# A two-layer decoder trunk on one core: first loads in another order and partly held back, last product in three parts, one selector matmul per forgetting head

## The chip, the cores and the metric

One core of one Trainium2 chip. The metric is the device time in microseconds (us) of one execution, the median of the runs shown. One execution was also taken by the hardware profiler; all views below come from it. Engines are named as in the profile: PE (TensorE matmul) and PEld (its weight load), DVE (VectorE), ACT (ScalarE), POOL (GpSimd), SP (SyncE, which issues DMAs).

## The reference, cut to what matters

Inputs are float32; 256 tokens (`SEQ`), width 2048 (`D_MODEL`), two layers. Each layer adds a mixer and an MLP to the residual `x`.

```python
def reference(x, ...):
    for i in range(2):
        h = rms_norm(x, mix_norm_g[i])
        # layer 0: forgetting attention, 16 heads of 128; layer 1: dilated attention, 8 heads x 3 groups
        mix = fox_attention(h, ...) if i == 0 else dilated_attention(h, ...)
        x = x + mix
        h = rms_norm(x, mlp_norm_g[i])
        x = x + sq_relu_mlp(h, mlp_w_up[i], mlp_w_down[i])      # (relu(h @ up) ** 2) @ down, d_ff 8192

def fox_attention(h, w_in, b_f, q_gain, k_gain, w_out):
    q, k, v, f = jnp.split(h @ w_in, [2048, 4096, 6144], axis=-1)    # f: one column per head
    q, k = rms_norm(q, q_gain), rms_norm(k, k_gain)                  # per head
    c = jnp.cumsum(jax.nn.log_sigmoid(f + b_f), axis=1)
    s = q @ k.T * 128 ** -0.5 + c[query] - c[key]                    # per head, causal
    return (softmax(s) @ v) @ w_out
```

## The kernel before, in words

**Products.** Every matrix product has float32 accuracy by parts: a weight tile is cast to a rounded part `wh` (ACT, line 279) and a remainder `wl` (DVE, line 280), the activations `hT` likewise (lines 370, 371), and `product` (lines 297 to 315) issues three matmuls for each of 16 `k` (128 rows of the contraction) and each of two blocks of 128 tokens: high by high, high by low, low by high (lines 308, 309, 310), each 128x128 by 128x512. One product is 96 matmuls over 512 output columns. `product_transposed` does the MLP's up half with swapped operands.

**Weights.** `plan` lists all weight tiles in order of use, 256 rows by 512 columns (512 KB, two `k`). `load` issues one DMA for each on SP's queue into one of five `raw` buffers, `split` casts it into one of five `wh`/`wl` pairs. After every second `k`, `product` calls `split` for a tile five ahead, so the streams run ahead of PE by a fixed depth.

**Order.** `Jobs` runs generators at ticks (one tick per `k`). A generator issues a step, yields a number of ticks or a key, and so is woven between matmuls. `behind(...)` holds instructions back in a scheduler's order until others are issued. The scheduler of the framework then fixes one instruction order per engine; each engine works strictly in that order.

**Start.** `load_x` brings `x` in four chunks of 512 columns (`xt[0..3]`), the first in two halves by columns. `gain_rows` and `gain_columns` bring the norm's gains and turn them to columns with one PE transpose. `norm_chain` for tag `n0`, for each chunk: four transposes for each half chunk (line 365, tile `ptx_n`), then ACT and DVE make the two parts of `hT` from PSUM with the gains (two PSUM buffers `ps_tp`, so the third group waits for the first to be read), and later ACT squares `x` for the row sums (line 381) that give `rstd`. The row scale is put on behind the product. `wake` issues idle transposes on PE. `more_constants` brings the forget-gate columns `wf` (128x16 rows of 64 bytes, line 160), the bias and the other gains. `rest` fills the weight pipeline. The first product is q of heads 0 to 3; then `gate` (line 522, tile `pf`), then k, then v. `gate_chain` turns the gate's sums into `c_q` and `negc`, the negated cumulative sums by head, as two parts on partitions 0 to 15 and 32 to 47.

**Forgetting heads.** `fox_head` builds a head's scores in one PSUM bank: columns 0 to 127 for the first token block (queries 0 to 127, 128 keys), columns 128 to 383 for the second (256 keys). Each block is its score matmuls (`scores`, lines 504 and 507) plus one matmul of a selector `sel` by `negc` (line 596), which adds the head's -c to all rows.

**End.** The last product (`out_proj` of the last MLP block, n = 3) runs both token blocks side by side through all 16 `k`; then `add_chain` adds each block to `x` (line 694) and `store` writes 256 KB for each block on SP's queue (line 708).

Of the kernel before, what the change touches and what calls it, by code (L numbers as in the profile page):

```python
# [17 lines left out]
P = 128  # L18
# [69 lines left out]
def trunk(ctx: ExitStack, tc, x, fox_w_in, fox_b_f, fox_q_gain, fox_k_gain, fox_w_out, dil_w_in,  # L88
# [34 lines left out]

    def gain_rows(name, sources):
        rows = work.tile([2 * KC, P], F32, tag="s", name=name, bufs=4)
        at = 0
        for src in sources:
            nc.sync.dma_start(rows[at:at + src.shape[0], :], src)
            at += src.shape[0]
        return rows[0:at, :]  # L130
# [6 lines left out]

    per_chunk = "l (c p) -> (l c) p"
    mix_rows = gain_rows("g_mix", [mix_norm_g.rearrange(per_chunk, p=P)])


# [15 lines left out]
    def more_constants():  # L157
        yield 6
        wf = work.tile([P, KC, FH], F32, tag="t2", name="wf")
        nc.sync.dma_start(wf, fox_w_in[0][:, 3 * D:3 * D + FH].rearrange("(c p) n -> p c n", p=P))  # L160
        nc.sync.dma_start(bf, fox_b_f.to_broadcast([P, FH]))
        qk_rows = gain_rows("g_qk", [fox_q_gain, fox_k_gain, dil_q_gain[0], dil_k_gain[0]])
        mlp_rows = gain_rows("g_mlp", [mlp_norm_g.rearrange(per_chunk, p=P)])
# [79 lines left out]
    def behind(*instructions):  # L243
# [3 lines left out]
        return stack  # L247

    state = {"raw": 0, "split": 0}
    raws, splits = [], []  # L250

    def load():
        i = state["raw"]
        if i >= len(plan):
            return
        w, r, cols = plan[i]
        t = wpool.tile([P, RAW_SUB, NC], F32, tag="raw", name=f"raw{i}", bufs=RAW_BUFS)
        at = 0
        for c, width in cols:
            nc.sync.dma_start(  # L260
                t[:, :, at:at + width],
                w[r:r + RAW_SUB * P, c:c + width].rearrange("(c p) n -> p c n", p=P),
            )
            at += width
        raws.append(t)
        state["raw"] += 1

    def split():
        i = state["split"]
        per = RAW_SUB // W_SUB  # L270
        if i >= len(plan) * per:
            return
        if i % per == 0:
# [4 lines left out]
        with behind(*(issued.get("n0", []) if i < 2 * W_BUFS else [])):  # L278
            nc.scalar.copy(hi, raw)  # L279
            nc.vector.tensor_sub(lo, raw, hi.bitcast(F32))  # L280
        splits.append((hi, lo))
# [4 lines left out]
    def in_turn(w, apart=NC // 2):  # L286
        return w.rearrange("p (b h n) -> p b n h", n=apart, h=2)
# [9 lines left out]
    def product(keys, lhs, post):  # L297

        acc = [ps_acc.tile([P, NC], F32, tag="acc", name=f"acc{used[0]}_{t}") for t in range(NT)]
        for k in range(KC):  # L300
# [13 lines left out]
            jobs.tick()  # L314
        jobs.spawn(post(acc))

    def product_transposed(keys, both, banks, post):
# [38 lines left out]
    def norm_chain(tag, col, n, ssp, wait, later):  # L356
        yield wait
        for half in range(2):
            pr = n * 2 + half
            pt = ps_tp.tile([P, 2, S], F32, tag="tp", name=f"ptx_{tag}_{pr}")  # L360
            with behind(*([issued["product"]] if wait else [])):
                for i in range(2):
# [12 lines left out]
            jobs.done.add((tag, pr))  # L375
            yield min(wait, 1)
        yield later
        with behind(issued[tag, n * 2 + 1][0]):
            for t in range(NT):
# [120 lines left out]

    def scores(ps, t, q, k, i, stop):
        (q_whole, q_hi, q_lo), (k_whole, k_hi, k_lo) = q, k
        if t == 0:
            nc.tensor.matmul(ps[:, 0:P], q_whole[:, i, :], k_whole[:, i, :], start=True, stop=stop)
            return
        for x, (a, b) in enumerate(((q_hi, k_hi), (q_hi, k_lo), (q_lo, k_hi))):
            nc.tensor.matmul(ps[:, P:3 * P], a[:, i, :], in_turn(b[:, i, :], P // 2), start=x == 0, stop=stop and x == 2)

# [6 lines left out]
    c_q = const.tile([P, NT, FH], F32, name="c_q")  # L515
    negc = const.tile([P, S], F32R, name="negc")

# [7 lines left out]
    def gate_chain(tag, pf):  # L525
# [50 lines left out]
        nc.vector.tensor_scalar(ct, pct, -1.0, None, ALU.mult)  # L576
        zero = work.tile([P, S], F32, tag="s", name="g_zero", bufs=4)
        nc.vector.memset(zero, 0.0)
        nc.vector.tensor_copy(negc, zero)
        nc.vector.tensor_copy(negc[0:FH, :], ct)  # L580
        nc.vector.tensor_sub(negc[32:32 + FH, :], ct, negc[0:FH, :].bitcast(F32))
        jobs.done.add("gate")

    def fox_head(j, hh, qT, kT, vt, sel):
# [5 lines left out]
        yield 2 * hh + 2  # L590
        ps = ps_sc.tile([P, 512], F32, tag="sc", name=f"sc_f{h}")
        for t in range(NT):
            at = ps[:, t * P:t * P + (t + 1) * P]
            n = (t + 1) * P
            scores(ps, t, qT[hh // 2], kT[hh // 2], hh % 2, False)
            nc.tensor.matmul(at, sel[:, hh, :], negc[:, 0:n], start=False, stop=True)
        s = work.tile([P, 3 * P], F32, tag="s", name=f"s_f{h}", bufs=4)
# [38 lines left out]
    def dil_head(q4, i, qTs, kTs, vt):  # L636
# [5 lines left out]
        for g in range(3):  # L642
            yield ("table", g)
            ps = ps_sc.tile([P, 512], F32, tag="sc", name=f"sc_d{h}_{g}")
            for t in range(NT):
                scores(ps, t, qTs[g], kTs[g], i, True)
            slope = 2.0 ** (-8.0 * (g * DH + h + 1) / N_SLOPES)
# [41 lines left out]
    def add_chain(acc, n, then, ready, scale):  # L689
# [11 lines left out]
        yield 0  # L701

    def out_proj(keys, lhs, then=None, ready=None, scale=None):
        for n in range(NX):
            product(keys, lhs, lambda acc, n=n: add_chain(acc, n, then, ready, scale))

# [48 lines left out]

    first = normed("n0", 0, lambda n: (0, 1, 4, 8)[n], lambda n: 11 - 3 * n)

    def load_x(n):
        step = NC if n else NC // 2
        for c in range(0, NC, step):  # L760
            nc.sync.dma_start(xt[n][:, :, c:c + step], xv[:, :, n * NC + c:n * NC + c + step])

    def rest():
        load_x(2)
        yield 2
        split()
        load_x(3)
        while state["split"] - used[0] < W_BUFS:
            split()
            yield 1  # L770

    load_x(0)
    gain_columns("g_mix", mix_rows, 0)
    jobs.spawn(first(0))
    with behind(issued["transposed"]):
        wake(12)
    for i in range(4):
        split()
        if i == 1:
            load_x(1)  # L780
    for n in range(1, NX):
# [64 lines left out]
```

## Time and profile before

| | |
|---|---|
| time, median of 3 runs | 2191.28 us (2191.07 to 2192.96) |
| the profiled execution | 2193.09 us, of which the span is 2191.4 us |
| mean granted PE clock | 0.998 |
| PE busy | 2179.7 us, 99% of the span |
| DVE busy | 1373.8 us, 63% |
| ACT busy | 1100.3 us, 50% |
| DMA | 425.76 MB, mean 194 GB/s |
| matmul 128x128 by 128x512, record / distance of starts | 0.38 us / 0.216 us |
| cast of one weight tile, ACT line 279 / DVE line 280 | 1.05 us / 1.23 us |

How to read it: a PE record overlaps the next one, so the work of PE is counted by the distance of starts. A timeline row gives start, duration, engine, line, operation, tiles, shape and count; at its end in brackets the idle time before it and who ended it. PEclk is the clock granted to PE as a share of full speed.

### The profile page before, as it was taken

The page shows a single profiled execution, that of the slowest core. Times are in us where ns is not written, and L with a number is a line of the kernel's source. Part 1 is how long each engine was busy: PE and PEld are TensorE (multiplying, and loading weights), DVE is VectorE, ACT ScalarE, POOL GpSimd, SP SyncE. Part 2 cuts the span into 40 slices and gives each one's busy share as a digit, 9 for nine tenths or more (in the row PEclk, how much of TensorE's full clock was granted, in tenths as well). Part 3 has the DMA queues.
Part 4 walks back from the last instruction along what each step waited for, and adds up shares of the span by engine and source line. Part 5 has one row for each costly group of instructions (what it writes and reads, how often), then busy time and mean ns, then how long its engine had stood idle before and what let it go on. Part 6 is the DMA issues. An engine that isn't in the chain of part 4 may idle for free.

```text
span 2191.4 us, 29887 instructions
## 1 busy us (share of the span) xinstructions
PE 2179.7 (99%) x11441; PEld 1939.3 (88%) x11441; DVE 1373.8 (63%) x1799; ACT 1100.3 (50%) x1516; POOL 48.2 (2%) x51
## 2 busy tenths in 40 slices
PE   8999999999999999999999999999999999999999
PEld 7888888998998998998888888888988988988988
DVE  6776686665565565565666767665655655665564
ACT  5655555554454454455555555555544544544442
POOL 1011000000000000000000000000000000000000
PEclk9999999999999999999999999999999999999999
DMA  7565556666766766765665565656666766666664
GB/s 228 170 192 173 182 167 200 197 202 203 202 203 203 201 203 203 201 202 194 192 200 174 178 189 172 199 175 189 206 203 201 202 202 202 201 203 203 201 212 144
DMA packets 248687, 425.76 MB, mean 194 GB/s; under 512 B 16792, under 2 KB 66528, under 8 KB 248544
## 3 DMA queue, kind: packets, MB, share of 16 engines
q1 hardware_dynamic: 248544, 423.86, 62.7%
q8 instruction: 89, 1.46, 0.3%
q14 instruction: 54, 0.44, 0.1%
HBM read 421.70 MB, written 2.10 MB: 193 GB/s over the span
## 4 chain that ended last, share of the span: by engine, by line
PE 98%; DVE 1%; DMA 0%; issue 0%; ACT 0%; SPq 0%; DVEq 0%; ACTq 0%
PE acc L308 21%; PE acc L309 21%; PE acc L310 21%; PE up_n1a_acc L329 5%; PE up_n3a_acc L329 5%; PE up_n1a_sc L329 3%; PE up_n1a_tp L329 3%; PE up_n3a_sc L329 3%; PE up_n3a_tp L329 3%; PE up_n3a_acc L333 3%; PE up_n1a_acc L333 3%; PE up_n3a_sc L333 1%; PE up_n3a_tp L333 1%; PE up_n1a_tp L333 1%; PE up_n1a_sc L333 1%; PE ptx_n L365 1%
## 5 line engine op out<-in xcount | busy, mean ns | idle before, releaser
L280 DVE TENSOR_TENSOR wl<-raw,wh 128x1024 fp32r<-128x1024 f32 x800 | 979.4, 1225 | 713.4 <-ACT wh L279 706.5
L279 ACT CAST wh<-raw 128x1024 fp32r<-128x1024 f32 x800 | 839.5, 1049 | 889.0 <-PE acc L310 528.5
L308 PE MATMUL acc<-wh,hT_n 128*128 128x512 f32 x896 | 347.1, 388 | 2.1 <-ACT wh L279 2.1
L309 PE MATMUL acc<-wl,hT_n 128*128 128x512 f32 x896 | 340.8, 380 | 0.1
L310 PE MATMUL acc<-wh,hT_n 128*128 128x512 f32 x896 | 340.7, 380 | 0.0
L308 PE MATMUL acc<-wh,aTh_n1a 128*128 128x512 f32 x512 | 194.5, 380 | 0.0
L309 PE MATMUL acc<-wl,aTh_n1a 128*128 128x512 f32 x512 | 194.0, 379 | 0.0
L310 PE MATMUL acc<-wh,aTl_n1a 128*128 128x512 f32 x512 | 194.0, 379 | 0.0
L308 PE MATMUL acc<-wh,aTh_n3a 128*128 128x512 f32 x512 | 194.0, 379 | 0.0
L309 PE MATMUL acc<-wl,aTh_n3a 128*128 128x512 f32 x512 | 194.0, 379 | 0.0
L310 PE MATMUL acc<-wh,aTl_n3a 128*128 128x512 f32 x512 | 194.0, 379 | 0.0
L310 PEld LDWEIGHTS acc<-wh,hT_n 128*128 128x128 f32 x896 | 169.9, 190 | 24.0
L308 PEld LDWEIGHTS acc<-wh,hT_n 128*128 128x128 f32 x896 | 169.9, 190 | 23.3 <-ACT wh L279 2.3
L309 PEld LDWEIGHTS acc<-wl,hT_n 128*128 128x128 f32 x896 | 170.2, 190 | 21.7 <-DVE wl L280 0.8
L329 PE MATMUL up_n3a_acc<-hT_n,wh 128*128 128x512 f32 x512 | 181.6, 382 | 0.0
L329 PE MATMUL up_n1a_acc<-hT_n,wh 128*128 128x512 f32 x512 | 181.6, 382 | 0.0
L333 PE MATMUL up_n1a_acc<-hT_n,wl 128*128 128x256 f32 x512 | 139.6, 273 | 0.0
L333 PE MATMUL up_n3a_acc<-hT_n,wl 128*128 128x256 f32 x512 | 139.6, 273 | 0.0
L310 PEld LDWEIGHTS acc<-wh,aTl_n1a 128*128 128x128 f32 x512 | 96.8, 189 | 13.7
L310 PEld LDWEIGHTS acc<-wh,aTl_n3a 128*128 128x128 f32 x512 | 96.8, 189 | 13.7
L309 PEld LDWEIGHTS acc<-wl,aTh_n3a 128*128 128x128 f32 x512 | 96.8, 189 | 13.7
L308 PEld LDWEIGHTS acc<-wh,aTh_n3a 128*128 128x128 f32 x512 | 96.8, 189 | 13.7
(721 smaller groups left out, 3161.4 us busy)
## 6 DMA issues: line engine op xcount, KB each, us to landing
raw<-in_mlp_w_up_dram SPq DMA_DIRECT2D x256, 512.0 KB, 4.4
raw<-in_mlp_w_down_dram SPq DMA_DIRECT2D x256, 512.0 KB, 4.1
raw<-in_fox_w_in_dram SPq DMA_DIRECT2D x96, 512.0 KB, 3.8
raw<-in_dil_w_in_dram SPq DMA_DIRECT2D x192, 256.0 KB, 3.1
raw<-in_fox_w_out_dram SPq DMA_DIRECT2D x32, 512.0 KB, 3.8
raw<-in_dil_w_in_dram SPq DMA_DIRECT2D x32, 512.0 KB, 3.8
raw<-in_dil_w_out_dram SPq DMA_DIRECT2D x32, 512.0 KB, 3.6
out_dram<-x SPq DMA_DIRECT2D x8, 256.0 KB, 5.6
```

Of the source, the lines that this page charges most:

```text
L279: nc.scalar.copy(hi, raw)
L280: nc.vector.tensor_sub(lo, raw, hi.bitcast(F32))
L308: nc.tensor.matmul(acc[t], ah[:, tok], hi, start=first, stop=False)
L309: nc.tensor.matmul(acc[t], ah[:, tok], lo, start=False, stop=False)
L310: issued["product"] = nc.tensor.matmul(acc[t], al[:, tok], hi, start=False, stop=last)
L329: issued["product"] = nc.tensor.matmul(banks[b], hi[:, i, col], in_turn(tokens.rearrange("p x s -> p (x s)"), P // 2), start=first, stop=last)
L333: nc.tensor.matmul(banks[b][:, 0:S], lo[:, i, col], in_turn(tokens[:, 0, :], P // 2), start=False, stop=False)
L365: issued["transposed"] = nc.tensor.transpose(pt[:, i, t * P:(t + 1) * P], xt[n][:, t, c:c + P], ident)
```

## The change

Four things are edited, all in one diff.

1. The first loads. `x`'s first chunk is loaded by token blocks, one on SP's queue and one on ACT's; the first weight tile likewise, its two `k` on two queues. The norm's gains come over POOL's queue. All later loads of the start (weight tiles 1 to 4 and `x` chunks 1 to 3, in turn) are held: DVE writes one column of each destination behind the gains' copy, and the DMA waits for that write (`hold`). `wf` and the other constants are issued later. The transposes of all chunks are placed behind the product's matmuls, the squares behind the latest cast, with other ticks; `wake(12)` becomes `wake(3)`. The first weight tile is cast in two halves.
2. `negc` holds 384 columns: the keys of the first block and then of both, in an interleaved order.
3. A head adds it with one selector matmul of 384 columns ahead of its scores.
4. The last product runs in three parts (token block 0, then the two column halves of token block 1): side by side for `k` 0 to 7, then one part after another for `k` 8 to 15, each with its own add and store.

The instructions' order on each engine behind the first forgetting heads, up to the last product, stays as it was but for a few neighbours that swap.

```diff
+    mix_rows = gain_rows("g_mix", [...], nc.gpsimd)
...
     def more_constants():
-        yield 6
+        yield 9
         wf = work.tile([P, KC, FH], F32, tag="t2", name="wf")
-        nc.sync.dma_start(wf, ...)
+        with behind(issued["load"]):
+            nc.sync.dma_start(wf, ...)            # and bf, g_qk, g_mlp
...
+    def hold(first):
+        if "held" not in issued:
+            return ExitStack()
+        with behind(issued["gained"]):
+            nc.vector.memset(first, 0.0)
+        return behind(*([issued["load"]] if issued["held"] == [] else []))
...
     def load():
+            src = w[r:r + RAW_SUB * P, c:c + width].rearrange("(c p) n -> p c n", p=P)
+            if i:
+                with hold(t[:, 0, 0:1]):
+                    issued["load"] = nc.sync.dma_start(t[:, :, at:at + width], src)
+            else:
+                for part, queue in enumerate((nc.sync, nc.scalar)):
+                    queue.dma_start(t[:, part, at:at + width], src[:, part, :])
...
+    def last_product(keys, lhs, ready):
+        parts = [(0, slice(0, NC)), (1, slice(0, S)), (1, slice(S, NC))]
+        acc = [ps_acc.tile([P, NC], F32, tag="acc", name=f"last{x}") for x in range(len(parts))]
+        begin = used[0]
+        steps = [(k, x) for k in range(KC // 2) for x in range(len(parts))]
+        steps += [(k, x) for x in range(len(parts)) for k in range(KC // 2, KC)]
+        for k, x in steps:
+            ...
+            nc.tensor.matmul(to, ah[:, tok], hi, start=first, stop=False)
+            nc.tensor.matmul(to, ah[:, tok], lo, start=False, stop=False)
+            nc.tensor.matmul(to, al[:, tok], hi, start=False, stop=last)
+            if last:
+                ready(to, t, cols)
...
     def norm_chain(tag, col, n, ssp, wait, later):
-            with behind(*([issued["product"]] if wait else [])):
+            with behind(*([issued["product"]] if "product" in issued else [])):
...
-        with behind(issued[tag, n * 2 + 1][0]):
+        with behind(issued["cast"]):              # the squares
...
     def fox_head(j, hh, qT, kT, vt, sel):
-        for t in range(NT):
-            at = ps[:, t * P:t * P + (t + 1) * P]
-            n = (t + 1) * P
-            scores(ps, t, qT[hh // 2], kT[hh // 2], hh % 2, False)
-            nc.tensor.matmul(at, sel[:, hh, :], negc[:, 0:n], start=False, stop=True)
+        nc.tensor.matmul(ps[:, 0:3 * P], sel[:, hh, :], in_turn(negc, P // 2), start=True, stop=False)
+        for t in range(NT):
+            scores(ps, t, qT[hh // 2], kT[hh // 2], hh % 2, True)
...
+    def final_add(n, tag):
+        def ready(acc, t, cols):
+            at = halves(xt[n][:, t, :])[:, 0, :, cols.start // 2:cols.stop // 2]
+            sums = acc.rearrange("p (n h) -> p h n", h=2)
+            nc.vector.scalar_tensor_tensor(at, sums, rstd[tag, 2][:, t:t + 1], at, ALU.mult, ALU.add)
+            dst = out[0][t * P:(t + 1) * P, n * NC:(n + 1) * NC].rearrange("p (h n) -> p h n", h=2)
+            (nc.scalar if cols.start else nc.sync).dma_start(dst[:, :, cols.start // 2:cols.stop // 2], at)
+        return ready
...
-    first = normed("n0", 0, lambda n: (0, 1, 4, 8)[n], lambda n: 11 - 3 * n)
+    first = normed("n0", 0, lambda n: (0, 2, 6, 10)[n], lambda n: (13, 11, 9, 7)[n])
...
+    load_x(0)                                     # block 0 on SP, block 1 on ACT
+    load()
+    gained = gain_columns("g_mix", mix_rows, 0)
+    issued["gained"] = gained
+    issued["held"] = True
+    for what in (load, lambda: load_x(1), load, lambda: load_x(2), load, lambda: load_x(3), load):
+        what()
+        issued["held"] = []
+    del issued["held"]
     jobs.spawn(first(0))
     with behind(issued["transposed"]):
-        wake(12)
+        wake(3)
```

More of the change, by code (lines that the diff above doesn't have):

```diff
@@ L122, in trunk, with gain_rows @@
     MLP_G, FOX_G, DIL_G = 2 * KC, 4 * KC, 4 * KC + 2
-    def gain_rows(name, sources):
+    def gain_rows(name, sources, queue=nc.sync):
         rows = work.tile([2 * KC, P], F32, tag="s", name=name, bufs=4)
@@ L127, in gain_rows @@
         for src in sources:
-            nc.sync.dma_start(rows[at:at + src.shape[0], :], src)
+            queue.dma_start(rows[at:at + src.shape[0], :], src)
             at += src.shape[0]
@@ L272, in split @@
             return
-        if i % per == 0:
+        if i % per == 0 and state["raw"] <= i // per:
             load()
@@ L277, in split @@
         lo = wpool.tile([P, W_SUB, NC], F32R, tag="wl", name=f"wl{i}", bufs=W_BUFS)
-        with behind(*(issued.get("n0", []) if i < 2 * W_BUFS else [])):
-            nc.scalar.copy(hi, raw)
-            nc.vector.tensor_sub(lo, raw, hi.bitcast(F32))
+        with behind(*([issued["gained"]] if i == 0 else issued.get("n0", []) if i < 2 * W_BUFS else [])):
+            for part in ([slice(0, 1), slice(1, 2)] if i < 1 else [slice(0, W_SUB)]):
+                issued["cast"] = nc.scalar.copy(hi[:, part, :], raw[:, part, :])
+                nc.vector.tensor_sub(lo[:, part, :], raw[:, part, :], hi[:, part, :].bitcast(F32))
         splits.append((hi, lo))
@@ L515, in trunk @@
     c_q = const.tile([P, NT, FH], F32, name="c_q")
-    negc = const.tile([P, S], F32R, name="negc")
+    negc = const.tile([P, 3 * P], F32R, name="negc")
     def gate(tag):
@@ L576, in gate_chain @@
         nc.vector.tensor_scalar(ct, pct, -1.0, None, ALU.mult)
-        zero = work.tile([P, S], F32, tag="s", name="g_zero", bufs=4)
+        zero = work.tile([P, 3 * P], F32, tag="s", name="g_zero", bufs=4)
         nc.vector.memset(zero, 0.0)
         nc.vector.tensor_copy(negc, zero)
-        nc.vector.tensor_copy(negc[0:FH, :], ct)
-        nc.vector.tensor_sub(negc[32:32 + FH, :], ct, negc[0:FH, :].bitcast(F32))
+        keys = by_column(ct, P // 2)
+        high, low = (negc[at:at + FH, :] for at in (0, 32))
+        nc.vector.tensor_copy(halves(high[:, P:], P // 2), keys)
+        nc.vector.tensor_sub(halves(low[:, P:], P // 2), keys, halves(high[:, P:], P // 2).bitcast(F32))
+        for part in (high, low):
+            nc.vector.tensor_copy(part[:, 0:P], part[:, P:2 * P].bitcast(F32))
         jobs.done.add("gate")
```

56 lines of the change are left out of this document (30 added, 26 removed).

## The prediction

> **What bounds the kernel now.** I read the page first, its chain of what ended last.
>
> ```profile
> PE 98%; DVE 1%; DMA 0%; issue 0%; ACT 0%; SPq 0%; DVEq 0%; ACTq 0%
> ```
>
> PE is the bound from end to end. So an edit is worth what it takes off PE's row of starts, where PE waits, or at either end. The waits of PE over the whole span name two of over 1 us behind the first loads, both before 28 us. So I read PE's timeline for the start, and the windows for the granted clock.
>
> ```profile
> 9.91 1.19 PE L308 MATMUL acc<-wh,hT_n 128*128 128x512 f32 x2 [2.06 <-ACT wh L279]
> ...
> 24.47 0.38 PE L310 MATMUL acc<-wh,hT_n 128*128 128x512 f32 x1
> 27.28 1.08 PE L365 MATMUL ptx_n<-ident,x 128*128 128x128 f32 x4 [2.43 <-issue]
> ...
> 40.82 3.81 PE L522 MATMUL pf<-hT_n,wfs 128*32 128x256 f32 x32
> ```
>
> ```profile
> 10.00:12.00 2.00, 1.94 (x4) 1.12 (x5) 1.87 (x2) 1.05 (x1) 0.00 (x0) 0.50 1.06 398
> ...
> 28.00:30.00 2.00, 2.00 (x7) 1.64 (x6) 1.48 (x2) 2.00 (x5) 0.00 (x0) 0.50 0.86 269
> ```
>
> The first product runs from 9.91 to 40.82 (the gate's start), 30.9 us. Its work is 96 matmuls at 0.216 = 20.7, six groups of transposes at 0.44 (30.50 to 30.95) = 2.6, two gain transposes 0.6: 23.9. So 7.0 are lost: 1.8 at the first six matmuls (9.91 to 13.04 for 1.3), 0.9 in small waits up to 20.7, 2.6 of standstill before 27.28, 1.5 at half clock behind it, 0.2 elsewhere. Half clock (0.50 in the column behind POOL's) follows each standstill of over 2 us and lasts some 3.4 us.
>
> Why PE stood still: ACT's and SP's timelines, and DMA's bytes in 40 slices of 1 us.
>
> ```profile
> 8.80 0.70 SPq L160 DMA_DIRECT2D wf<-in_fox_w_in_dram  x1
> ```
>
> ```profile
> 21.91 1.05 ACT L279 CAST wh<-raw 128x1024 fp32r<-128x1024 f32 x1 [3.00 <-DMA raw<-in_fox_w_in_dram]
> ...
> 24.24 0.47 ACT L370 ACTIVATE hT_n<-ptx_n,gain 128x256 fp32r<-128x256 f32 x1
> ```
>
> ```profile
> GB/s 0 10 152 327 128 131 236 385 401 410 404 393 383 389 381 384 238 95 46 213 238 401 404 315 68 336 193 166 186 352 418 379 379 326 315 59 135 348 59 244
> ```
>
> `wf`, 2048 rows of 64 bytes, goes ahead of weight tile 5; while it moves (16 to 19 us) the rate falls to 46. Tile 5 comes late, ACT waits 3.00 for it in order, the reading of `ptx_n` lies behind that on ACT, and the seventh group of transposes waits for the PSUM buffer.
>
> **The change part by part.**
>
> A, the first matmul. Before, 1.04 MB (gains, `x` chunk 0, tile 0) are through by 7.1 us (sum of the slices), but tile 0 lands only at 8.8, since later tiles share the engines. After, these 1.04 MB are alone, on two queues; the second half of tile 0 waits on ACT's queue for the table load and the first activation (1.28 + 0.20). It lands between 5.0 (ramp overlapped with `x`) and 7.6 (the same slices plus 0.5 for completion); I take 6.3, nearer to the slices. Then ACT: half cast 0.55, `hT` 0.47, 0.1 for signals: first matmul at 7.45, which is 2.5 earlier (1.2 to 3.7).
>
> B, the first product. It now holds seven groups (3.1) and one gain transpose (0.3): 24.1. `wf` is behind tile 8, so the 2.6 and 1.5 go. What is late next: tile 1. Its DMA waits for the gains, the gains' transpose stands on PE behind `wake(8)` and its POOL DMA, and DVE's seven column writes behind it: issue at about 5.1. Before, packets follow an issue by about 1.2 and the first tiles take 2 to 2.5 while the rate is at 130; so tile 1 lands at 9 to 9.5, and PE needs it cast (1.05) at 10.5. The casts and `hT` alternate on ACT, 2.0 us for 3.0 of PE, so behind tile 2 PE leads no more waits. I charge either one spell of half clock (1.7) or that first chain (1.0): 1.3, and 0.7 for a tile 1 or `x` chunk 1 that is late. End of the product 7.45 + 24.1 + 2.0 = 33.5 in place of 40.8: 7.3 gained (4 to 9). Half-clock matmuls cover the same waits, so the two aren't added.
>
> C, the gate in the second product. The squares of `x`, and with them `rstd`, come later: the scheduled order puts them into the k product, and puts the cumulative-sum matmuls (line 611) into `k` 14, where before they came after `k` 10. They wait for a DVE chain. ACT has the gate's exponential behind a cast that waits for PE's `k` 9 to free its buffer (13.6 us after the product starts, cast to 14.6); DVE's remainder of that tile runs to 15.8; then fifteen small DVE steps (3.1 us up to a remainder of 1.23 that waits for `k` 11, then 1.7): 21.9. PE is there at 20.6. So PE waits 1.3, and 0.3 more for the copy between the sums and their transpose: 1.6 lost (0 to 3.5). All matmuls behind stand in that queue. Under 2 us of standstill I charge no half clock.
>
> D, the heads. Before, one head's eight starts run
>
> ```profile
> 82.50 0.38 PE L504 MATMUL sc_f<-fkT_0w,fqT_0w 128*128 128x128 f32 x2
> 82.64 0.30 PE L596 MATMUL sc_f<-negc,sel 128*128 128x128 f32 x1
> 82.78 0.33 PE L507 MATMUL sc_f<-fkT_0h,fqT_0h 128*128 128x256 f32 x1
> ...
> 83.17 0.28 PE L596 MATMUL sc_f<-negc,sel 128*128 128x256 f32 x1
> 83.29 0.38 PE L308 MATMUL acc<-wh,hT_n 128*128 128x512 f32 x1
> ```
>
> from 82.50 to 83.29: 0.79. A dilated head, the same scores with no selector, takes 0.55 (1328.21 to 1328.76). A matmul of 384 columns is 0.75 of 0.216 = 0.16. So 0.79 - 0.71 = 0.08 for each of 16 heads: 1.2 gained (0.4 to 2). The extra DVE copies into `negc` (0.3 to 0.4 each, three more) end well before the heads at `k` 12 of v.
>
> E, the end. Matmuls of 256 columns cost 0.112 (twelve pairs of 512 and 256 in the MLP's up half take 3.93), 0.004 over half a 512: 96 of them, 0.4 lost. The tail:
>
> ```profile
> 2186.81 1.41 DVE L694 SCALAR_TENSOR_TENSOR x<-acc,rstd_n,x 128x512 f32<-128x512 f32 x2 [10.00 <-PE acc L310]
> ...
> 2187.04 0.38 PE L310 MATMUL acc<-wh,aTl_n3a 128*128 128x512 f32 x1
> 2187.59 0.99 SPq L708 DMA_DIRECT2D out_dram<-x  x2
> ```
>
> The last add halves (0.70 to about 0.4, the 256-column row of DVE's score adds being 0.41 in the mean), and 128 KB is left to store in place of two 256 KB that share the engines (0.5 MB at 390 GB/s is 1.3): 0.7 gained. Net 0.3 gained (-0.5 to 1.0). The third accumulator takes the buffer of product n = 2, whose add ends 0.5 after that product; PE is there 1.0 after it, so no wait. The last weight tile is cast 4 us before part one needs it.
>
> Sum: -7.3 + 1.6 - 1.2 - 0.3 = -7.2 on a span of 2191.4. The profiled execution took 2193.09, 1.7 outside the span, and lies 1.8 above the median; the change is within the span, so against the median 2191.28 it gives 2184.1.
>
> The page "TensorE: Matmul & The Clock Gate" of the Trainium skill (Part 1, on the clock gate and its oscillation) has a free-running activity window of about 3.4 us and sets the limit for PE's idle gaps at about as much. Here gaps of 2.06 and 2.6 already brought the half clock, for about the window that it names; the trace decides. By the page alone the wait in C would be safe even at twice its size, and the sum would stay 2184.1.
>
> **The rivals.**
>
> 1. Two queues bring nothing: the transfers share the same engines, the first matmul stays near 9.9, and only the removed standstill counts. For it: DMA ran near 400 GB/s from 7 to 16 us, so there is no free rate later; against it: at 4 to 6 us it ran at 130. Then A's 2.5 goes: 2186.6. The Trainium skill's page "DMA: Bandwidth & Descriptors" (Rules for kernel authors) says this: spreading DMAs over issuing engines saves issue time alone, and splitting a transfer by halves is no help. No run here shows two queues yet. Chance 0.10.
>
> 2. The gate's chain in C costs over 2 us and brings a half-clock spell: 3.5 and 1.7 in place of 1.6, so 3.6 worse: 2187.7. For it: PE leads by 7 us there, while DVE's chain depends on casts that wait for PE. Against it: DVE is idle a fifth of that stretch. Chance 0.12.
>
> 3. Slower: all held loads hang on one 16 KB load of the gains by POOL's queue, which no row of this trace prices. It is free until the gains arrive at about 5; each us later moves tile 1 and PE by 1 us, and at 12 the 7.2 are eaten, at 16.7 it is 4.4 slower: 2195.7. From below, SP's own gains load was there by 3.8; from above, the longest landing of a start load was 10.7. Taken near SP's, as it is as small. Chance 0.06, with all that ends slower.
>
> 4. Nothing measurable: the DMA ramp of 130 GB/s comes back at every held load, so that PE starves through the product and gets back a third: 2189. Chance 0.04.
>
> **How the numbers follow.** The forecast has 0.68 and runs from 2181 to 2186.9. A measurement of this kernel can tell a change from none at about 0.2%, 4.4 us, so same is 2186.9 to 2195.7. Faster: 0.68, rival 1 nearly whole, little of rival 2: 0.77. Same: 0.16. Slower: 0.07. The range reaches down to 2180.8 (A and B at their best, C at 1) and up to 2189.8 (rivals 1, 2 and 4).
>
> **What would show it.** PE's first line 322 matmul (line 308 before) at about 7.5, in any case before 9; the gate (line 565) at 33 to 35; no DMA wait of ACT over 1 us on a weight tile after 12 us; a PE wait of 0.5 to 3 us at lines 610 to 617; a head's starts within 0.72; a last add of 0.4 and a tail from last matmul to end near 3.6 in place of 4.4. Wrong would be a first matmul past 9.9, a second stretch at half clock, or starts of the 256-column matmuls of the last product over 0.13 apart.

## The result, and the profile after

The changed kernel takes 2186.35 us (median of 10 runs, 2186.11 to 2186.94). Ten runs of the kernel before beside it have a median of 2191.99 us. The ratio is 0.9975, 95% interval 0.9965 to 0.9984: 5.6 us faster, where 7.2 were forecast. The profiled executions differ by 6.3 in their spans: 2191.4 and 2185.1.

The ten runs of the kernel before fall into two groups of five, 2191.07 to 2191.43 and 2192.56 to 2192.96, between which their median lies, and its profiled execution (2193.09) is of the upper one; the runs of the changed kernel fall into one.

The chain that ended last still is PE's.

```profile
PE 98%; DVE 1%; ACT 0%; issue 0%; DMA 0%; POOL 0%; ACTq 0%; POOLq 0%
```

PE's timeline for the start, with the gate's first matmul at the end (start, duration, engine, line, tiles, shape, count; in brackets the idle time before and its releaser):

```profile
6.36 0.31 PE L135 MATMUL ps_g_mix<-ident,g_mix 32*128 32x32 f32 x1 [1.85 <-DMA g_mix<-in_mix_norm_g_dram]
...
8.28 0.80 PE L322 MATMUL acc<-wh,hT_n 128*128 128x512 f32 x1
8.87 0.63 PE L323 MATMUL acc<-wl,hT_n 128*128 128x512 f32 x1
...
11.00 0.87 PE L406 MATMUL ptx_n<-ident,x 128*128 128x128 f32 x4
...
34.88 3.90 PE L565 MATMUL pf<-hT_n,wfs 128*32 128x256 f32 x32
```

The first product matmul starts at 8.28 (before 9.91, forecast 7.45), the gate at 34.88 (before 40.82, forecast 33.5). What set the first of them are the gains: PE waits for them up to 6.36, though ACT could cast tile 0 at 5.83 already, and the transposes and `hT` come behind the gains. SP's timeline shows the same from the other side: the held loads, behind the gains' copy and the column writes, are issued from 6.95 on.

```profile
5.83 1.14 ACT L293 CAST wh<-raw 128x512 fp32r<-128x512 f32 x2 [3.08 <-DMA raw<-in_fox_w_in_dram]
```

```profile
6.95 0.38 SPq L272 DMA_DIRECT2D raw<-in_fox_w_in_dram  x1
```

In DMA's bytes (GB/s in 40 slices of 1 us) the price of the hold is the gap from 6 to 8 us, 0 and 10:

```profile
GB/s 0 10 221 264 375 195 0 10 139 258 234 373 383 399 418 348 387 406 399 391 385 387 391 378 187 42 10 28 123 254 311 410 383 393 408 381 385 125 203 287
```

After 14.6 us PE's row has no gap up to the gate: the standstill of 2.6 and the half clock behind it are gone. The first six matmuls are still 0.43 apart (the first two 0.59), and yet the windows give a granted clock (the column behind POOL's) of 1.00:

```profile
8.00:10.00 2.00, 2.00 (x6) 1.45 (x5) 1.22 (x3) 0.70 (x2) 0.00 (x0) 1.00 0.84 199
```

So at the start the column doesn't tell of the pace; the distance of starts does.

The wait in the gate's chain, a head, and the end (PE, then DVE's last add and ACT's last store):

```profile
59.88 0.36 PE L610 MATMUL pc<-g_lf,tri 128*128 128x16 f32 x2 [0.21 <-DVE g_lf L607]
```

```profile
77.48 0.33 PE L639 MATMUL sc_f<-negc,sel 128*128 128x384 f32 x1
77.64 0.39 PE L546 MATMUL sc_f<-fkT_0w,fqT_0w 128*128 128x128 f32 x2
...
78.09 0.28 PE L549 MATMUL sc_f<-fkT_0h,fqT_0l 128*128 128x256 f32 x1
78.20 0.38 PE L322 MATMUL acc<-wh,hT_n 128*128 128x512 f32 x1
```

```profile
2181.36 0.28 PE L350 MATMUL last<-wh,aTl_n3a 128*128 128x256 f32 x1
2181.68 0.48 DVE L752 SCALAR_TENSOR_TENSOR x<-last,rstd_n,x 128x256 f32<-128x256 f32 x1 [2.20 <-PE last L350]
2182.19 0.40 ACTq L754 DMA_DIRECT2D out_dram<-x  x1
```

The head takes 78.20 - 77.48 = 0.72 (before 0.79). The tail from the last matmul's start to the end is 2185.1 - 2181.36 = 3.74 (before 4.36).

Where the 6.3 us of the span came from, by distances between the same points in both traces:

| stretch | before | after | difference |
|---|---|---|---|
| start to gate | 40.82 | 34.88 | -5.94 |
| gate to first head | 41.68 | 42.60 | +0.92 |
| first head to last matmul | 2104.54 | 2103.88 | -0.66 |
| last matmul to end | 4.36 | 3.74 | -0.62 |

### The profile page after: what moved, and what is told of

It is laid out like the page before. It is cut to its first block, busy times and chain, and to the rows that moved or that the text cites. A ratio compares the mean times of both kernels' runs of the same rounds, so it can differ in the third digit from the quotient of the medians.

```text
span 2185.1 us, 29948 instructions
## 1 busy us (share of the span) xinstructions
PE 2175.9 (100%) x11464; PEld 1937.9 (89%) x11464; DVE 1372.8 (63%) x1810; ACT 1099.9 (50%) x1517; POOL 49.3 (2%) x52
## 4 chain that ended last, share of the span: by engine, by line
PE 98%; DVE 1%; ACT 0%; issue 0%; DMA 0%; POOL 0%; ACTq 0%; POOLq 0%
PE acc L322 21%; PE acc L324 21%; PE acc L323 21%; PE up_n3a_acc L370 5%; PE up_n1a_acc L370 5%; PE up_n3a_tp L370 3%; PE up_n3a_sc L370 3%; PE up_n1a_sc L370 3%; PE up_n1a_tp L370 3%; PE up_n1a_acc L374 3%; PE up_n3a_acc L374 3%; PE up_n1a_tp L374 1%; PE up_n1a_sc L374 1%; PE up_n3a_sc L374 1%; PE up_n3a_tp L374 1%; PE ptx_n L406 1%
## 5 line engine op out<-in xcount | busy, mean ns | idle before, releaser
L294 DVE TENSOR_TENSOR wl<-raw,wh 128x1024 fp32r<-128x1024 f32 (+1 forms) x801 | 978.7, 1223 | 703.8 <-ACT wh L293 697.0
L293 ACT CAST wh<-raw 128x1024 fp32r<-128x1024 f32 (+1 forms) x801 | 838.4, 1047 | 881.9 <-PE acc L324 525.8
L322 PEld LDWEIGHTS acc<-wh,hT_n 128*128 128x128 f32 x896 | 169.6, 190 | 21.9 <-ACT wh L293 0.6
L322 PE MATMUL acc<-wh,aTh_n3a 128*128 128x512 f32 x480 | 181.9, 379 | 0.0
L323 PE MATMUL acc<-wl,aTh_n3a 128*128 128x512 f32 x480 | 181.9, 379 | 0.0
L324 PE MATMUL acc<-wh,aTl_n3a 128*128 128x512 f32 x480 | 181.9, 379 | 0.0
L323 PEld LDWEIGHTS acc<-wl,aTh_n1a 128*128 128x128 f32 x512 | 96.8, 189 | 13.6
L370 PEld LDWEIGHTS up_n1a_acc<-hT_n,wh 128*128 128x128 f32 x512 | 96.8, 189 | 13.5
L322 PEld LDWEIGHTS acc<-wh,aTh_n1a 128*128 128x128 f32 x512 | 96.8, 189 | 13.5
```

The lines of the kernel that those rows point to most:

```text
L293: issued["cast"] = nc.scalar.copy(hi[:, part, :], raw[:, part, :])
L294: nc.vector.tensor_sub(lo[:, part, :], raw[:, part, :], hi[:, part, :].bitcast(F32))
L322: nc.tensor.matmul(acc[t], ah[:, tok], hi, start=first, stop=False)
L323: nc.tensor.matmul(acc[t], ah[:, tok], lo, start=False, stop=False)
L324: issued["product"] = nc.tensor.matmul(acc[t], al[:, tok], hi, start=False, stop=last)
L370: issued["product"] = nc.tensor.matmul(banks[b], hi[:, i, col], in_turn(tokens.rearrange("p x s -> p (x s)"), P // 2), start=first, stop=last)
```

## The experiments

My theory after the result: the start gained what it did because the standstill behind tile 5 went, and lost 1.4 us of the forecast to the gains on POOL's queue; the heads and the end brought what was forecast. The rivals: the start's half clock, the old place of `wf`, the hold, and the second queue. Runs 1 to 4, 5 to 8 and 9 to 11 each share the runs of the kernel before that stand beside them; where others are set side by side, it is by their ratios.

### 1. Heads and end alone

```diff
 the kernel before; of the change only:
+    negc = const.tile([P, 3 * P], F32R, name="negc")        # and its filling
+        nc.tensor.matmul(ps[:, 0:3 * P], sel[:, hh, :], in_turn(negc, P // 2), start=True, stop=False)
+                last_product(keys, lhs, final_add(n, scale))
```

> The kernel before with parts 2 to 4 of the change alone (the selector matmul of 384 columns, the last product by parts); the start stays as before. Theory (terms D and E simply add): a head's starts take 0.71-0.72 us in place of 0.79, so the last product starts 1.1-1.2 us earlier against the first head; the end from last matmul to span end falls by 0.6-0.7 and the 256-column matmuls give 0.4 back. Span 1.4 us under the one before: 2190.0 from 2191.4; the gate's start stays near 40.8. Rival (the heads are bound by what comes behind their scores, the end by the stores): the starts shorten but the distance from the first head to the last product does not, span within 0.4 of before.

Measured: ratio 0.9995 (0.9986 to 1.0004), median 2191.64 beside 2192.71; span 2188.7. PE's timeline:

```profile
11.46 0.38 PE L310 MATMUL acc<-wh,hT_n 128*128 128x512 f32 x1
11.68 0.38 PE L309 MATMUL acc<-wl,hT_n 128*128 128x512 f32 x1
...
18.23 0.63 PE L392 MATMUL ptx_n<-ident,x 128*128 128x128 f32 x4 [1.19 <-issue]
...
27.34 0.63 PE L392 MATMUL ptx_n<-ident,x 128*128 128x128 f32 x4 [2.51 <-issue]
...
29.10 0.60 PE L392 MATMUL ptx_n<-ident,x 128*128 128x128 f32 x4
...
39.33 3.87 PE L550 MATMUL pf<-hT_n,wfs 128*32 128x256 f32 x32
```

First head to last matmul takes 2103.90 (81.08 to 2184.98), the tail 3.72: 0.64 and 0.64 less than before, 1.28 in all where 1.4 was expected. The rival falls by these distances; the ratio's interval reaches past 1, so by the times alone the gain is not shown. The rest of the span's 2.7 isn't the edit's: with the very start of the kernel before, this execution (2190.39, the lower of two groups here as well: 2190.2 to 2190.44 and 2191.58 to 2192.24) shows 0.216 in its first matmuls and no half clock behind the standstill, and the gate at 39.33 in place of 40.82. So 1.5 us of the old profile was half clock that other executions of the same start don't have. All of it lies behind the standstill: from the seventh group of transposes to the eighth PE takes 1.76 here (27.34 to 29.10) and took 3.31 before (27.28 to 30.59). The half clock at the first matmuls cost nothing by itself: at full pace PE only waits 1.19 for the fifth group, which starts at 18.23 in place of 18.25.

### 2. The gains by SP's queue

```diff
-    mix_rows = gain_rows("g_mix", [...], nc.gpsimd)
+    mix_rows = gain_rows("g_mix", [...], nc.sync)
```

> The changed kernel with the gains loaded by SP's queue ahead of everything else in place of POOL's queue. Theory G (the gains' arrival at 6.3 sets the first matmul and the release of the held loads): gains on PE at about 4.0 as in the kernel before (3.83), the seven column writes at about 4.4, held loads issued from about 4.5 in place of 6.95; then tile 0 (cast from 5.83) sets the first matmul, at 6.8 to 7.4 in place of 8.28; gate at 33.0 to 34.0 in place of 34.88; span 1.0 to 1.8 us shorter than the changed kernel's 2185.1. Rival (tile 0 and x set it, and the hold protects them): held loads issued at 4.5 share the engines with tile 0, which lands after 7; first matmul at 8 or later, gate within 0.4 of 34.88, span within 0.5.

Measured: ratio 0.9976 (0.9967 to 0.9986), the changed kernel's own within the uncertainty; span 2184.7. The gains were on PE at 3.82, the held loads went out early, and the rival came true:

```profile
8.52 0.79 PE L322 MATMUL acc<-wh,hT_n 128*128 128x512 f32 x1 [0.40 <-ACT hT_n L411]
```

`x` came only at 6.37 and tile 0 was cast from 6.96 on (5.83 in the changed kernel). The held loads went out from 4.41, ahead of `x`'s landing; in run 11, below, they are released by `x` itself at 4.96, and tile 0 is cast from 5.79. That they shared the engines with what is needed first is the likeliest reason.

### 3. `wf` in its old place

```diff
-        yield 9
+        yield 1
         wf = ...
         with behind(issued["load"]):
             nc.sync.dma_start(wf, ...)
+        yield 8
+        with behind(issued["load"]):
             nc.sync.dma_start(bf, ...)            # and g_qk, g_mlp
```

> The changed kernel with wf alone moved back to its old place on SP's queue, between weight tiles 4 and 5 (the other constants stay behind tile 8). Theory W (wf's 2048 rows of 64 bytes made tile 5 late, and so the standstill of 2.6 us and the 1.5 us at half clock): the DMA rate falls under 150 GB/s for 1 to 2 us, ACT waits 1 us or more for a weight tile, PE stands still for 1 to 2.6 us in the first product, the gate starts at 36.5 to 39 in place of 34.88, span 1.6 to 4 us longer than 2185.1. Rival (the old order of x and weight tiles caused it; with x loaded in turn there is a lead of a tile or more): PE waits under 0.5 us more, gate at 34.9 to 35.4, span within 0.5.

Measured: ratio 0.9978 (0.9969 to 0.9987), span 2185.1, the gate at 34.80. DMA's slices and ACT's timeline:

```profile
GB/s 0 12 190 299 369 195 0 10 145 252 248 373 354 404 406 373 393 401 332 109 96 238 277 406 401 404 280 36 30 193 305 291 225 328 363 401 387 373 274 305
```

```profile
24.10 1.04 ACT L295 CAST wh<-raw 128x1024 fp32r<-128x1024 f32 x1 [1.49 <-DMA raw<-in_fox_w_in_dram]
```

The rate falls to 96 and tile 5 is late, as theory W says, though by half as much (a wait of 1.49 in place of 3.00); but PE doesn't notice. In the new order the reading of the transposes stands ahead of that cast on ACT, and the cast alone is in time. My theory that `wf` as such cost the standstill falls for the changed kernel.

### 4. No hold

```diff
     def hold(first):
-        if "held" not in issued:
+        if True:
             return ExitStack()
```

> The changed kernel without the hold: no column writes, all later loads are issued on SP's queue one behind another from about 1.7 us on; the order of the loads is the changed one. Theory H (the hold is what gives x chunk 0 and tile 0 the engines alone): tile 0 lands at 8 to 9 as in the kernel before (8.8), first matmul at 9.3 to 10, gate at 35.5 to 36.5, span 0.6 to 1.6 us longer than 2185.1. Rival (the gains by POOL's queue set the first matmul anyway, and the hold only leaves the DMA engines idle from 6 to 8 us): first matmul at 8.3 or up to 0.5 later, the later tiles come 3 us earlier, the small waits of PE up to 14.6 us (1.0 together) go, gate at 33.5 to 34.8, span 0.1 to 1.3 us shorter.

Measured: ratio 0.9985 (0.9976 to 0.9994), median 2188.98 beside 2192.71; span 2187.3, 2.2 longer than with the hold. The hold is worth more than theory H gave it, and in part for another reason: not tile 0 comes last (cast from 7.08) but the gains, which compete as well.

```profile
7.67 0.31 PE L135 MATMUL ps_g_mix<-ident,g_mix 32*128 32x32 f32 x1 [3.17 <-DMA g_mix<-in_mix_norm_g_dram]
```

First matmul at 9.60, gate at 37.11.

### 5. The kernel before with `wf` late

```diff
 the kernel before
-        yield 6
+        yield 9
+        with behind(issued["load"]):
             nc.sync.dma_start(wf, ...)            # and bf, g_qk, g_mlp
```

> The kernel before with one edit: wf and the other constants go behind weight tile 8 (before: wf between tiles 4 and 5). Theory 'either one suffices' (the standstill of 2.4 to 2.5 us in the kernel before needs both a late tile 5 and ACT's order, in which the reading of the transposes stands behind that tile's cast): tile 5 now comes 1.5 us or more earlier, ACT waits under 1.5 us for it, PE's standstill near 27 us falls under 1 us, gate at 36.5 to 38.8 where the old start gave 39.3 (no half clock) or 40.8 (with it). Theory 'wf plays no part' (the order of transposes on ACT alone): ACT's wait of 3.0 us and PE's of 2.4 us stay, gate at 39 to 41.

Measured: ratio 0.9984 (0.9975 to 0.9993), median 2188.89 beside 2192.79: 3.9 us by this edit alone. ACT waits 0.79 for tile 5 in place of 3.00, and PE's standstill at the seventh transposes is gone (ACT's row, then PE's):

```profile
19.66 1.05 ACT L280 CAST wh<-raw 128x1024 fp32r<-128x1024 f32 x1 [0.79 <-DMA raw<-in_fox_w_in_dram]
```

```profile
25.03 0.63 PE L366 MATMUL ptx_n<-ident,x 128*128 128x128 f32 x4 [0.22 <-PE acc L311]
```

The gate starts at 36.54, though this execution has half clock at the first matmuls (0.50 and 0.67 in the windows from 10 to 14 us). So either remedy suffices, `wf` late in the old start (this run) or the new start with `wf` early (run 3). That the second works by ACT's order, in which PE's transposes are read ahead of the late cast, is read from run 3's trace; no run changes that order alone, and the new start also has `x` in turn with the tiles.

### 6. Dummies up to the gains

```diff
-    wake(8)
+    wake(16)
```

> The changed kernel with 16 dummy transposes in place of 8 ahead of the gains, so that PE works without a gap from 2.54 up to about 6.4. Theory K (the 0.43 distance of the first six matmuls, 8.28 to 11.0, is half clock brought by PE's idle 1.85 us before the gains): the first six matmuls are 0.216 to 0.25 apart, first product ends 1.0 to 1.4 us earlier, gate at 33.5 to 33.9 in place of 34.88, span 2183.7 to 2184.1. Rival (tile 1 and x chunk 1 come too late for PE to use the time: ACT casts tile 1 from 12.28 on): the matmuls are faster but PE waits at 12 to 14.6 us for as much longer; gate within 0.4 of 34.88, span within 0.5 of 2185.1.

Measured: median 2186.36, ratio 0.9974 (0.9963 to 0.9984), span 2185.3. PE's idle before the gains is filled, and the pace stays 0.43 up to 11.7:

```profile
2.54 3.68 PE L116 MATMUL spare<-ident 128*128 128x128 f32 x16 [2.54 <-POOL ident masks.py:199]
...
10.15 1.06 PE L324 MATMUL acc<-wh,hT_n 128*128 128x512 f32 x2
11.00 1.06 PE L406 MATMUL ptx_n<-ident,x 128*128 128x128 f32 x4
```

Theory K falls: PE's idle time ahead of the gains isn't what makes the pace low. The rival's figures hold (gate at 35.07, span 2185.3) but not its reason, as the matmuls weren't faster.

### 7 and 9. The gains on ACT's queue, with 14 dummies and with 8

```diff
-    mix_rows = gain_rows("g_mix", [...], nc.gpsimd)
 ...
     load_x(0)
+    mix_rows = gain_rows("g_mix", [...], nc.scalar)
     load()
 run 7 besides: wake(14) for wake(8)
```

> The changed kernel with the gains on ACT's queue between x's second block and the second half of tile 0 (in place of POOL's queue), and 14 dummy transposes in place of 8. Theory: gains land at about 5 with x, held loads are issued at about 5.5 in place of 6.95, tile 0 is cast from 5.9 to 6.3 as its half goes 0.4 later, first matmul at 6.9 to 7.5 in place of 8.28, at full clock; gate at 32.5 to 33.6, span 2182.7 to 2183.8: the best of all. Rival (as with the gains by SP: x and tile 0 come later by what the gains and the held loads take): x after 6 and tile 0 at 6.8 to 7.2, first matmul at 8.0 to 8.6, only the clock is gained: gate at 33.3 to 34.3.

> The run with gains on ACT's queue and 14 dummy transposes, with the dummy transposes back at 8: gains on ACT's queue alone. It parts that run's 1.2 us (gate 33.64 in place of 34.88) into gains and clock. Theory: the gains bring 0.7 (first matmul at 7.5 to 7.7), and the six first matmuls stay 0.43 apart as in all runs with 8 dummies: gate at 33.9 to 34.3, span 2184.1 to 2184.6. Rival (the dummies play no part): gate at 33.5 to 33.8, span 2183.5 to 2183.9.

Measured: medians 2185.44 and 2185.41 beside 2192.79, ratios 0.9969 (0.9958 to 0.9981) and 0.9968 (0.9956 to 0.9981); spans 2183.7 and 2183.5. With 8 dummies:

```profile
5.60 0.31 PE L135 MATMUL ps_g_mix<-ident,g_mix 32*128 32x32 f32 x1 [1.71 <-DMA g_mix<-in_mix_norm_g_dram]
...
7.52 0.80 PE L321 MATMUL acc<-wh,hT_n 128*128 128x512 f32 x1
...
33.43 3.83 PE L564 MATMUL pf<-hT_n,wfs 128*32 128x256 f32 x32
```

The gains 0.76 earlier bring the first matmul 0.76 earlier and the gate 1.45 earlier, a part of it because the pace of 0.43 ends sooner (at 9.4; in the changed kernel behind 11.0). The dummies play no part. The gate at 33.43 is just ahead of the rival's range. The first matmul at 7.52 and the gate at 33.43 are what was forecast for the changed kernel (7.45 and 33.5), though the held loads go out at 6.19, 1.1 later than forecast. With 14 dummies the first matmul is at 7.57 and the gate at 33.64, both just past that run's theory, on the side of its rival.

### 8. One queue

```diff
-                queue = nc.scalar if t == 1 else nc.sync
+                queue = nc.sync
 ...
-                for part, queue in enumerate((nc.sync, nc.scalar)):
+                for part, queue in enumerate((nc.sync, nc.sync)):
```

> The changed kernel with both blocks of x's first chunk and both halves of tile 0 on SP's queue (gains still by POOL's queue, hold as changed). Theory S (the hold and the gains' arrival matter, the second queue does not): tile 0 cast from 5.8 to 6.8, still ahead of the gains' 6.3 plus transposes and copy (hT at 7.75); first matmul at 8.2 to 8.5, span within 0.4 of 2185.1. Rival (two queues bring the early landing): tile 0 cast from 7.3 or later, first matmul at 8.8 or later, gate 0.5 to 1.5 later than 34.88, span longer by as much.

Measured: median 2186.04 beside 2192.79, ratio 0.9971 (0.996 to 0.9982), span 2184.5. Tile 0 is cast from 6.14 (5.83 on two queues), and the gains come earlier, at 5.53; first matmul at 7.77, gate at 34.26. The second queue brings 0.3 on tile 0, which in the changed kernel waits for the gains anyway, and there the gains come 0.83 later than here. By the two profiled executions one queue is 0.6 shorter; the ratios' intervals overlap, so that is not shown.

### 10. Wide dummies

```diff
 run 9, with
-    wake(8)
+    for _ in range(10):
+        nc.tensor.matmul(wide, full[:, 0:P], full, start=True, stop=True)   # zeros, 128x512, fp32r
```

> Gains on ACT's queue, and in place of the 14 dummy transposes ten dummy matmuls of 128x512 (a tile of zeros, fp32r) ahead of the gains. Theory L (what raises the clock is how full PE's work is: 16 transposes of 128 columns at 0.23 from 2.54 to 6.22 left the clock low until 11.7): the wide dummies start at about 1.7 at 0.43, fall to 0.216 before 6, and the first six product matmuls are 0.216 to 0.25 apart; first matmul at 7.5, gate at 32.7 to 33.2, span 2182.8 to 2183.3. Rival M (the clock rises only at certain moments, whatever the work is): the first matmuls stay 0.43 apart for 1 us or more, gate at 33.5 to 34.3, span 2183.6 to 2184.4.

Measured: median 2185.85 beside 2192.79, ratio 0.997 (0.9958 to 0.9982), span 2184.6, gate at 34.44, later than either theory has it. The first six matmuls start within 8.47 to 9.87, 0.22 to 0.27 apart, earlier than in any run with dummy transposes behind a held start (9.4 to 12.2). That is theory L's pace. But the ten dummies ran at 0.43 up to 6.5 and made the gains wait, the held loads were issued at 7.14, and PE then waited 1.18 for tile 1's cast:

```profile
12.94 0.70 PE L327 MATMUL acc<-wh,hT_n 128*128 128x512 f32 x2 [1.18 <-ACT wh L298]
```

Here the full pace gained nothing: the next tile wasn't there.

### 11 and 12. Gains first on ACT's queue, the hold on `x`, then with wide dummies

```diff
 the changed kernel, x's first chunk and tile 0 on SP's queue (as in run 8), and
-    mix_rows = gain_rows("g_mix", [...], nc.gpsimd)
+    mix_rows = gain_rows("g_mix", [...], nc.scalar)
 ...
-            nc.vector.memset(first, 0.0)
+            nc.vector.tensor_scalar_mul(first, xt[0][:, 1, 0:1], 0.0)
 run 12 besides: four wide dummies for wake(8), four for wake(3)
```

> The changed kernel with the gains alone and first on ACT's queue, x's first chunk and tile 0 on SP's queue, and the held loads released by a column copied from x's second block (in place of a memset behind the gains). Theory: gains on PE at 3.9 to 4.5, x lands at 5.0 to 5.5 and sets the transposes, tile 0 is cast from 6.0 to 6.3, hT at 6.3 to 6.9, first matmul at 6.9 to 7.5; held loads issued at 5.2 to 6.0; the first six matmuls 0.43 apart; gate at 33.2 to 34.0, span 2183.4 to 2184.2. Rival (whatever is asked for early, the same engines carry it: x and tile 0 come later by as much): first matmul at 7.7 or later, gate at 34.2 or later, span over 2184.4.

Measured in run 11: median 2186.14 beside 2192.79, ratio 0.997 (0.9959 to 0.9982), span 2184.3. The held loads go out at 4.96, tile 0 is still cast from 5.79, the first matmul is at 7.45, all as the theory says or a little sooner; but the pace of 0.43 lasts up to 12.2, and the gate is at 34.24, as the rival has it.

> The run with the gains first on ACT's queue and the hold on x, with wide dummy matmuls (128x512) in place of the dummy transposes: four ahead of the gains (for eight), four behind the first transposes (for three). Theory L (full work raises the clock, and with held loads issued at 5 tile 1 lands by 9.8, so PE can use it): first matmul at 7.3 to 7.7, product matmuls 0.216 apart from 8.5 at the latest, PE waits under 0.6 in all before 15 us, gate at 32.0 to 33.0 in place of 34.24, span 2182.1 to 2183.1: the shortest of all. Rival (a bound by loads and casts, as in the run with ten wide dummies, where PE waited 1.18 for tile 1): PE waits over 0.8 for tile 1 or 2, gate at 33.2 to 34.2. Rival M (the clock's moments): the first matmuls stay 0.43 apart to 10 us or later, gate at 33.5 to 34.5.

Measured in run 12: median 2185.11 (2184.97 to 2185.22) beside 2192.11, ratio 0.9968 (0.9956 to 0.9981), span 2183.5.

```profile
7.62 0.48 PE L332 MATMUL acc<-wh,hT_n 128*128 128x512 f32 x1 [0.69 <-ACT hT_n L421]
...
9.12 0.38 PE L334 MATMUL acc<-wh,hT_n 128*128 128x512 f32 x1
...
12.21 0.63 PE L416 MATMUL ptx_n<-ident,x 128*128 128x128 f32 x4 [0.98 <-DMA x<-in_x_dram]
```

The records last 0.38 to 0.48 from the first matmul on (0.63 to 0.80 in the changed kernel), so the pace is full; what it gains PE loses at 12.21 to `x` chunk 1, issued at 5.45, and the gate is at 33.40. The pace is theory L's and the gate the first rival's, whose wait came for `x` and not for a tile. That the wide dummies brought the pace is not shown, since transposes alone did so in the kernel before: its 12 dummies behind the first transposes took 1.66, the same 12 in run 1 took 2.76 (before, then run 1):

```profile
6.19 1.66 PE L116 MATMUL spare<-ident 128*128 128x128 f32 x12
```

```profile
6.43 2.76 PE L116 MATMUL spare<-ident 128*128 128x128 f32 x12
```

Runs 7, 9 and 12 are the best found, by their medians about 1 us shorter than the changed kernel; their ratios to before (0.9968 and 0.9969) and its 0.9975 have intervals that overlap.

## Why the prediction was right, and where it wasn't

The direction and the main term were right, and the 5.6 us lie in the range. That it came so near is in part luck: the start brought 1.4 less than forecast, and the gate's chain made up for half of that by costing 0.7 less. Point by point:

- **A and B, -7.3 forecast, -5.94 measured.** The failing step is the one that put the gains "at about 5" and let the first matmul hang on tile 0 alone. Tile 0 came sooner than forecast (cast from 5.83; landing put at 6.3), the gains came at 6.3, the held loads at 6.95 in place of 5.1, the first matmul at 8.28 in place of 7.45. That is 0.8 of the 1.4; from there to the gate it took 26.6 in place of 26.05. Run 9, with the gains on ACT's queue, meets the forecast (7.52; 33.43), in part by luck, since its gains (5.60) and held loads (6.19) are still later than forecast and the slow pace ended sooner. So rival 3's mechanism is real and has cost up to 1.4 us of a gain, far from the 7.2 it would need. I priced the load by SP's, which goes ahead of all others: the gains took 4.9 us from issue to landing. POOL's queue is the smaller part of that. Beside the same loads ACT's queue had the gains on PE at 5.60 (run 9), and POOL's had them there at 5.53 with the other loads on one queue (run 8); ahead of everything they were there at 3.82, on SP's queue (run 2) and on ACT's (run 11).
- **The reason given for B was half of one.** "`wf` is behind tile 8, so the 2.6 and 1.5 go": run 5 shows that this does suffice in the old order (3.9 us), run 3 that the new start would have done without it. The prediction named ACT's order as a link of the chain and then charged only `wf`.
- **The half clock.** I compared with the median of three runs, 2191.28, and noted that the profiled execution was 1.8 above it, without asking why. That excess is half clock that the lower group lacks: beside run 1, each of the 18 runs of before from 2192.53 up has a mean granted clock of 0.998 or 0.999 and each of the 13 up to 2191.57 has 1.00 (in the later sets two of the lower runs read 0.999), and run 1's own trace shows where it lies (1.5 less at the gate). The 7.3 counts it as a gain. Against the lower group of before (2191.1) the change brings 4.8, against the upper (2192.8) 6.4. The rule that half clock follows each standstill of over 2 us, read from one execution, doesn't hold either: none followed 2.51 in run 1, and in run 5 it came behind 1.83 and a further 0.56. Nor were the 1.8 charged to the first six matmuls a loss that could be won back (run 1).
- **C, +1.6 forecast, +0.92 measured.** Of the wait at line 610 only 0.21 is left (1.3 forecast): DVE's chain took 21.1 us from the gate's end in place of 21.9, and PE was there at 20.9 in place of 20.6, since the second gain transpose (0.31) now stands in the second product. That transpose is a third of the 0.92; it only moved. Some 0.4 of the 0.92 is traced to no row here.
- **D and E, -1.5 forecast, -1.28 measured,** alike in run 1 and in the changed kernel. A head is 0.72; the last add 0.48 (0.4 forecast), the tail 3.74 (3.6).
- **Rival 1** had the mechanism right and the consequence wrong: the second queue isn't needed (run 8), but the first matmul came earlier all the same, because of the hold (run 4). Run 8, where tile 0 was cast 0.3 later and the gate came 0.6 sooner on one queue, agrees with the rule of the Trainium skill's page "DMA: Bandwidth & Descriptors" (Rules for kernel authors) that spreading DMAs over issuing engines saves issue time alone. **Rivals 2 and 4** didn't come: the wait in C is 0.21, and from 11 us on DMA stays above 340 GB/s until 24.
- **The range's lower end** was summed wrongly: A and B at 9 and C at 1 give 2181.8; 2180.8 needs C at nothing.

By the spans of the profiled executions the parts of the 6.3 are `wf` late 3.9 (run 5), heads and end 1.3 (run 1), and 1.1 left for all the rest of the new start, with C's loss in it. By the medians (3.9 and 1.1 of 5.6) 0.6 is left; but half clock in some executions moves each of these by up to 1.5, so the split is rough.

## What to carry over

When a start is bound by loads, ask which is the last thing that the first matmul and the release of the later loads hang on: here it was a load of 16 KB that landed behind the megabyte issued beside it, and moving that one load to another queue (run 9) brought the first matmul 0.76 us forward. Before a standstill is charged to the late transfer that ends it, look at what stands behind that transfer's consumer on the same engine; either may be enough to remedy it (runs 3 and 5). And if a profiled execution is longer than the median, find out first what it has that the others lack, since a forecast made from it counts that as gain.

## What was not expected of the hardware

- A 16 KB load by POOL's queue took 4.9 us from issue (1.40) to landing, and how long depends on what is issued beside it: it was on PE at 5.53 with the other first loads on one queue (run 8), at 6.36 with them on two (the changed kernel), at 7.67 without the hold (run 4). On SP's or ACT's queue ahead of everything it was on PE at 3.82 (runs 2 and 11).
- At the new start PE's pace was 0.43 per 128x512 matmul up to 9.4 to 13 us with dummy transposes before it, even without a gap ahead of the gains (run 6), and full behind dummy matmuls of 512 columns (runs 10 and 12), while the granted clock read 1.00 throughout. In the old start of the kernel before it was full from about 6.5 with transposes alone (its 12 dummies in 1.66 us). Each is one profiled execution, and the end of the slow pace moves by over 3 us among the runs with transposes; what sets its moment stays open. The page "TensorE: Matmul & The Clock Gate" of the Trainium skill (Part 1) speaks of a window of some 3.4 us; in run 6 3.68 us of transposes, and the work right behind them, didn't raise the pace before 11.7, so that window alone doesn't tell the moment here.
- The old start runs in two ways from one execution to the next, 1.5 us apart at the gate in the two traces, with 0.50 or 1.00 of the clock at the same places (10 to 14 and 28 to 30 us, kernel before and run 1).
